# Attention scores of two heads made together, the keys' low parts as two 64-row matmuls side by side in the array

## The chip, the cores and the metric

The kernel runs on one core of one Trainium2 chip. The metric is device time in microseconds (us) of one execution; less is better. In the profile PE is TensorE's matmul, PEld its weight load, DVE is VectorE, ACT is ScalarE, POOL is GpSimd and SP is SyncE. L966 is line 966 of the kernel.

## The reference

One decoder layer on 512 tokens of width 1024, in float32: a norm, one wide input projection, two token mixers side by side (causal pooling, and sparse attention), a gated merge with an output projection, and an MLP with a squared ReLU. The change lies in the attention: 16 heads of 64 channels, eight heads to a group that shares its keys and values. Each query has three branches, each with a softmax of its own: compressed keys (31 of them), selected blocks of 64 keys, and a sliding window. With 512 tokens there are 8 blocks and up to 16 are picked, and the window is 512 long, so that both the selected and the window branch see every earlier key.

```python
def nsa_mixer(q, kc, vc, ks, vs, kw, vw, g_nsa, ...):
    q = apply_rope(q.reshape(B, S, N_HEADS, dh), cos, sin).reshape(B, S, G, HPG, dh)
    ks = apply_rope(ks.reshape(B, S, G, dh), cos, sin)
    kw = apply_rope(kw.reshape(B, S, G, dh), cos, sin)
    ...
        s_s = jnp.einsum('bqghd,bgqkd->bghqk', qb, k_sel) * scale
        p_s = masked_softmax(s_s, ok[:, :, None])
        o_s = jnp.einsum('bghqk,bgqkd->bqghd', p_s, v_sel)
    ...
        s_w = jnp.einsum('bqghd,bkgd->bghqk', qb, kwb) * scale
        p_w = masked_softmax(s_w, wmask)
        o_w = jnp.einsum('bghqk,bkgd->bqghd', p_w, vwb)
        o = gb[..., 0:1] * o_c + gb[..., 1:2] * o_s + gb[..., 2:3] * o_w
```

## The kernel before

Matmuls run in the fp32r format. To keep float32's accuracy, an operand is split into a high part (the value rounded to fp32r) and a low part (the rest), and a product is the sum of high x high, high x low and low x high.

The kernel has three stages. Up to about 180 us it makes the norm, the pooling mixer, the compressed keys and values and part of the input projection. Then comes the attention. Behind it come the merge, the output projection and the MLP. Line 377 and line 1339 are helpers that issue the big projections' matmuls. At about 73 us the compressed branch adds two small transposes of 64 rows (line 698) and some plain float32 matmuls (line 707); at about 123 us there are matmuls with 64 columns of weights (line 722). A transpose of 36 rows at about 24 us (line 802) turns a few small inputs.

**The attention's work unit is a slot.** There are 96: for each of 8 pairs of heads 12 slots, in a fixed order written out by the list `slots`. A slot holds the pair `p`, the branch `br`, a block `qb` of 128 queries and the head `h` of the pair (0 or 1). For the first two query blocks one slot takes both branches; for the last two each branch has its own slot. Slots 2k and 2k+1 differ only in `h`.

**How a score is made.** For a pair of heads the tile `Q[p]` has 128 partitions. For `h` = 0 its rows 0 to 63 hold the query's high part and rows 64 to 127 its low part; for `h` = 1 it is the other way round (`q_done`). `KH[g]` holds the keys' high parts twice, in rows 0 to 63 and in rows 64 to 127, and `KL[g]` the keys' low parts in the same way (`k_done`). So one 128-row matmul with `KH` gives (query high + query low) x key high, and a second one with `KL` adds (query high + query low) x key low in the same PSUM bank. `score_pe` issues the two one after the other, with 256, 384 or 512 columns.

**What follows a score.** `smax` (line 988, DVE) takes the masked score out of PSUM and finds the row's extreme, `expo` (line 998, ACT) exponentiates, `weight` (lines 1008 and 1011, DVE and POOL) divides by the sum and multiplies by the gate, `turn_pe` (line 1028, PE) transposes the weights four slots later, `turn_hi` (line 1039, ACT) and `turn_lo` (line 1043, DVE) split them, and `pv` (line 1062, PE) multiplies by the values two slots after that, once for each two slots.

**The order** is one loop over the slots. Slot `i` of the loop issues in turn: the score of slot `i + 1`, the transposes of slot `i - 4`, the maximum, exponential and weight work, a step of the generators in `side` (rope, the compressed scores), the filler's matmuls up to an even share (`fill`, the projections of line 377 with the tile `psF`), and every second slot a `pv`. Instructions stay in about that order on each engine.

**Banks.** Scores rotate through three PSUM banks (`tag="S"`, `S_BANKS` = 3). The compressed scores of the next pair (`cmp_scores`, tile `psC`), which join `side` at slot 3 of every twelve, take a bank of the same three.

Of the kernel before, what the change touches and what calls it, by code (L numbers as in the profile page):

```python
# [13 lines left out]
F32 = mybir.dt.float32  # L14
# [6 lines left out]
S = 512  # L21
# [5 lines left out]
S_BANKS, T_BANKS, F_BANKS = 3, 2, 2  # L27
# [35 lines left out]
def trunk(ctx: ExitStack, tc: tile.TileContext, A, out):  # L63
    nc = tc.nc
    PE, ACT, DVE, POOL = nc.tensor, nc.scalar, nc.vector, nc.gpsimd
    PSUM = bass.MemoryType.PSUM

    def pool(name, **kw):
        return tc.tile_pool(name=name, bufs=1, reuse_waits="tile", **kw)
# [107 lines left out]
    for c in range(4):  # L177
# [7 lines left out]
        if c < C_FF2:  # L185
# [3 lines left out]
            for o in OUT_TURN:  # L189
                g = seen.get(o, 0)  # L190
# [68 lines left out]
    def add_sum(behind=None):  # L259

        to, _, q = jobs[begun.popleft()]
        with tc.issue_after(behind.ins) if behind else nullcontext():
            POOL.dma_start(to, q, accum_op=ALU.add)  # L263
# [129 lines left out]
    def step_side():  # L393
        for _ in range(len(side)):
            g = side.popleft()
            try:
                next(g)
                side.append(g)
            except StopIteration:
                pass  # L400
# [64 lines left out]
    KH = [ap.tile([128, 4, 2, 128], FR, name=f"KH{g}") for g in range(2)]  # L465
    KL = [ap.tile([128, 4, 2, 128], FR, name=f"KL{g}") for g in range(2)]
# [94 lines left out]
    scored = {"pairs": 0, "rope": 0}  # L561
# [44 lines left out]
    Q = {}  # L606
# [13 lines left out]
    with ExitStack() as c1:  # L620
# [185 lines left out]
        for k in P1[2:]:  # L806
            i = int(k[-1]) if k[-1].isdigit() else None
# [35 lines left out]
    with ExitStack() as c2:  # L843
        p2 = c2.enter_context(pool("p2"))
        ps2 = c2.enter_context(pool("ps2", space=PSUM))
# [43 lines left out]
        def fill(n=1):  # L889
            for _ in range(n):  # L890
                if next(filler, True):
                    return False
                fdone[0] += 1
            return True
# [46 lines left out]
        slots = []  # L941
# [9 lines left out]
        live = {}  # L951
        PT = {}
        O = {}

        def score_pe(i):
            p, half, br, qb, h = slots[i]
            g = p // 4
            nb = qb + 1
            ps = ps2.tile([128, S], F32, tag="S", bufs=S_BANKS, name="psS")
            q = Q[p][:, h, 128 * qb:128 * qb + 128]  # L960
            for K, a in ((KH[g], True), (KL[g], False)):
                if half == 0:
                    rhs, n = K[:, 0:nb, :, :], 256 * nb
                else:
                    rhs, n = K[:, 0:nb, br, :], 128 * nb
                PE.matmul(ps[:, 0:n], q, rhs, start=a, stop=not a, skip_group_check=True)  # L966
            live[i] = ps

        def blocks(i):
            p, half, br, qb, h = slots[i]  # L970
# [5 lines left out]
        def smax(i):  # L976
            p, half, br, qb, h = slots[i]
            ps = live[i]
            sm = p2.tile([128, 3, 2], F32, tag="sm", bufs=6, name="sm")
            P = p2.tile([128, S], F32, tag="P", bufs=P_BUFS, name="P")  # L980
            for e, (b, o, nb) in enumerate(blocks(i)):
                n = 128 * nb
                if half == 0:
                    s = ps[:, 0:2 * n].rearrange("p (a b c) -> p a b c", b=2, c=128)[:, :, b, :]
                else:
                    s = ps[:, 0:n].rearrange("p (a c) -> p a c", c=128)
                m = cmask[:, S - n:].rearrange("p (a c) -> p a c", c=128)
                DVE.tensor_tensor_reduce(out=P[:, o:o + n].rearrange("p (a c) -> p a c", c=128), in0=s, in1=m,  # L988
                                         scale=1.0, scalar=3e38, op0=ALU.add, op1=ALU.min,
                                         accum_out=sm[:, 0, e:e + 1])  # L990
            live[i] = (ps, sm, P)

        def expo(i):
            p, half, br, qb, h = slots[i]
            ps, sm, P = live[i]
            for e, (b, o, nb) in enumerate(blocks(i)):
                c = P[:, o:o + 128 * nb]
                last_exp[:] = [ACT.activation(c, c, AF.Exp, bias=sm[:, 0, e:e + 1], scale=-1.0,  # L998
                                              accum_out=sm[:, 1, e:e + 1])]

        def weight(i):
            p, half, br, qb, h = slots[i]
            ps, sm, P = live[i]
            head = 2 * p + h
            bl = blocks(i)
            nb_ = len(bl)
            c = 3 * head + 1 + bl[0][0]
            DVE.reciprocal(sm[:, 2, 0:nb_], sm[:, 1, 0:nb_])  # L1008
            for e, (b, o, nb) in enumerate(bl):
                n = 128 * nb  # L1010
                r = POOL.tensor_scalar(P[:, o:o + n], P[:, o:o + n], sm[:, 2, e:e + 1],  # L1011
                                       GT[:, qb, c + e:c + e + 1], op0=ALU.mult, op1=ALU.mult)
            return r
# [8 lines left out]
        def turn_pe(i):  # L1022
            p, half, br, qb, h = slots[i]
            ps, sm, P = live[i]
            n = sum(b[2] for b in blocks(i))
            pt = ps2.tile([128, S], F32, tag="T", bufs=T_BANKS, name="psT")
            for j in range(n):
                PE.transpose(pt[:, 128 * j:128 * j + 128], P[:, 128 * j:128 * j + 128], ident)  # L1028
            live[i] = (pt, n)

        def turn_views(i):
            h = slots[i][4]
            pt, n = live[i]
            tH, tL = pt_tile(i)
            return pt[:, 0:128 * n].rearrange("p (a c) -> p a c", c=128), tH[:, 0:n, h, :], tL[:, 0:n, h, :]

        def turn_hi(i):
            src, dH, dL = turn_views(i)
            ACT.activation(dH, src, AF.Copy)  # L1039

        def turn_lo(i):
            src, dH, dL = turn_views(i)
            DVE.tensor_tensor(dL, src, dH.bitcast(F32), op=ALU.subtract)  # L1043
            live.pop(i)

        def pv(i):
            p, half, br, qb, h = slots[i]
            g = p // 4
            if (p, half) not in O:
                O[p, half] = [ps2.tile([128, 2, 2, 128], F32, tag="O", bufs=1, name="psO"), 2 if half == 0 else 4]  # L1050
                c = PTc[p]
                for h in range(2):
                    PE.matmul(O[p, half][0][:, :, h, :], VC[g][h], c[:, 256 * half:256 * half + 256],
                              start=h == 0, stop=False, skip_group_check=True)
            ps = O[p, half][0]
            O[p, half][1] -= 1
            last = O[p, half][1] == 0
            tH, tL = PT.pop((p, br, qb))
            kbs = [(b, k) for b in ((0, 1) if br is None else (br,)) for k in range(qb + 1)]
            for j, (b, k) in enumerate(kbs):  # L1060
                for t in (tH, tL):
                    PE.matmul(ps[:, qb % 2, :, :], VV[:, k, b, g, :], t[:, j, :, :], start=False,  # L1062
                              stop=last and j == len(kbs) - 1 and t is tL, skip_group_check=True)
            return last
# [15 lines left out]
        n = len(slots)  # L1080
        total = 4 * len(FILL2) + 4
        done0 = fdone[0]
        after = deque()
        score_pe(0)
        for i in range(n + LAG + PLAG):
            if i < n:
                p = slots[i][0]
                if i % 12 == 3 and p + 1 < NPAIR:
                    while p + 1 not in Q:
                        fill()  # L1090
                        step_side()
                if i % 12 == CMP_AT and p + 1 < NPAIR:
                    side.append(cmp_scores(p + 1))
            if i + 1 < n:
                score_pe(i + 1)
                scored["pairs"] = (i + 2) // 12
            t = i - LAG
            if 0 <= t < n:
                turn_pe(t)
                turn_hi(t)  # L1100
            if i < n:
                smax(i)
                expo(i)
            if 0 <= i - 1 < n:
                last = weight(i - 1)
            if i % 4 == 3 and len(begun) > 1:
                add_sum(last)
            if 0 <= t < n:
                turn_lo(t)
            step_side()  # L1110
            want = done0 + (total - done0) * (i + 1) // (n + LAG + PLAG)
            while fdone[0] < want and fill():
                pass
            if i < 5:
                fill()
            j = t - PLAG
            if 0 <= j < n and j % 2 == 1 and pv(j):
                o_evac(*slots[j][0:2])
# [368 lines left out]
    for c in range(4):  # L1487
# [16 lines left out]
        if c < C_FF2:  # L1504
            outs = [Out(c, h, Y) for h in range(2)]
            seen = {}
            for o in OUT_TURN:
                h = seen.get(o, 0)
# [61 lines left out]
```

## Time and profile before

| | |
|---|---|
| median of 3 runs | 826.72 us (826.69 to 827.03) |
| profiled execution | 825.73 us, span 824.0 us |
| PE busy | 792.6 us (96%), 5081 matmuls |
| DVE busy | 615.0 us (75%) |
| ACT busy | 483.5 us (59%) |
| POOL busy | 206.1 us (25%) |
| score matmuls (line 966) | 96 with high keys, 96 with low keys, from 186.2 to 378.0 us |

A row of the profile names the line, the engine and the operation, then the tile written and the tiles read, then the shape. For a matmul `128*128 128x512` stands for 128 rows and 128 columns of weights in the array and 512 streamed columns; `64*128` means that 64 rows of the array are used. Matmuls are pipelined: the duration of one runs from its start to the (modelled) end of its result, and in a stream the next one starts well before that. What one costs in a stream is the distance from its start to the next start.

### The profile page before, as it was taken

The page shows a single profiled execution, that of the slowest core. Times are in us where ns is not written, and L with a number is a line of the kernel's source. Part 1 is how long each engine was busy: PE and PEld are TensorE (multiplying, and loading weights), DVE is VectorE, ACT ScalarE, POOL GpSimd, SP SyncE. Part 2 cuts the span into 40 slices and gives each one's busy share as a digit, 9 for nine tenths or more (in the row PEclk, how much of TensorE's full clock was granted, in tenths as well). Part 3 has the DMA queues.
Part 4 walks back from the last instruction along what each step waited for, and adds up shares of the span by engine and source line. Part 5 has one row for each costly group of instructions (what it writes and reads, how often), then busy time and mean ns, then how long its engine had stood idle before and what let it go on. Part 6 is the DMA issues. An engine that isn't in the chain of part 4 may idle for free.

```text
span 824.0 us, 13915 instructions
## 1 busy us (share of the span) xinstructions
PE 792.6 (96%) x5081; PEld 708.5 (86%) x5081; DVE 615.0 (75%) x1201; ACT 483.5 (59%) x959; POOL 206.1 (25%) x271
## 2 busy tenths in 40 slices
PE   7999999998899999999999999999999999899996
PEld 5889878886788888888787889999999999899985
DVE  6797744549979988888554689986898689987823
ACT  5566433327778787899323585933782468347711
POOL 6000000027767866674234101101101010000000
PEclk9999999999999999999999999999999999999999
DMA  9363732357446624554955709969996785245402
GB/s 299 97 173 109 201 85 89 109 154 163 68 127 117 146 73 92 101 129 109 297 157 160 173 1 274 296 171 248 264 255 153 232 231 179 93 139 179 154 1 102
DMA packets 121277, 127.71 MB, mean 155 GB/s; under 512 B 5077, under 2 KB 109049, under 8 KB 121082
## 3 DMA queue, kind: packets, MB, share of 16 engines
q1 hardware_dynamic: 101914, 107.17, 40.5%
q0 software_dynamic: 19008, 18.88, 16.3%
q8 instruction: 40, 0.66, 0.3%
q10 hardware_dynamic: 288, 0.79, 0.3%
q14 instruction: 27, 0.22, 0.1%
HBM read 122.09 MB, written 39.85 MB: 197 GB/s over the span
## 4 chain that ended last, share of the span: by engine, by line
PE 71%; DVE 16%; ACT 5%; issue 3%; DMA 2%; POOL 1%; SPq 0%; DVEq 0%; ACTq 0%; POOLq 0%
PE psF L377 21%; PE psB L1339 16%; PE psB L377 12%; PE psB L1455 9%; PE psO L1062 3%; PE psT L1028 3%; PE psS L966 2%; DVE wl L291 2%; PE psV L377 2%; DVE P L988 2%; DVE PT L1043 1%; DMA raw<-w_out 1%; PE psF L431 1%; ACT P L998 1%; PE psC L666 1%
## 5 line engine op out<-in xcount | busy, mean ns | idle before, releaser
L377 PE MATMUL psF<-R,wh 128*128 128x512 f32 x512 | 166.6, 404 | 0.2 <-ACT MA L824 0.2
L289 ACT ACTIVATE wh<-raw 128x1024 fp32r<-128x1024 f32 x66 | 69.8, 1057 | 80.6 <-PE psB L1339 29.1
L334 ACT ACTIVATE wh<-raw 128x512 fp32r<-128x512 f32 (+1 forms) x102 | 61.3, 619 | 86.8 <-PE psF L377 35.8
L377 PEld LDWEIGHTS psF<-R,wh 128*128 128x128 f32 x512 | 92.4, 189 | 17.9 <-ACT MA L824 0.5
L377 PE MATMUL psF<-R,wl 128*128 128x512 f32 x256 | 101.6, 397 | 0.7 <-DVE wl L336 0.7
L1011 POOL TENSOR_SCALAR P<-P,sm,GT 128x128 f32<-128x128 f32 (+3 forms) x128 | 85.6, 700 | 46.6 <-DVE sm L1008 31.0
L291 DVE TENSOR_TENSOR wl<-raw,wh 128x1024 fp32r<-128x1024 f32 x66 | 80.6, 1221 | 20.1 <-ACT wh L289 19.5
L263 POOL DMA_DIRECT2D S<-w_ff x36 | 41.7, 1159 | 213.2 <-DMA S<-w_ff 162.0
L336 DVE TENSOR_TENSOR wl<-raw,wh 128x512 fp32r<-128x512 f32 (+1 forms) x78 | 56.1, 731 | 37.3 <-ACT wh L334 36.9
L998 ACT ACTIVATE P<-P,sm 128x128 f32<-128x128 f32 (+3 forms) x128 | 71.0, 557 | 11.2 <-DVE sm L988 10.1
L1339 PE MATMUL psB<-R,wh 128*128 128x256 f32 x352 | 64.1, 282 | 0.0
L988 DVE CUSTOM_DVE_ANT_0 P<-psS,cst 128x128 f32<-128x128 f32 (+3 forms) x128 | 59.6, 483 | 5.9 <-PE psT L1028 4.2
L336 POOL TENSOR_TENSOR wl<-raw,wh 128x512 fp32r<-128x512 f32 x28 | 39.9, 1428 | 84.3 <-ACT wh L334 82.0
L1043 DVE TENSOR_TENSOR PT<-psT,PT 128x512 fp32r<-128x512 f32 (+2 forms) x96 | 56.7, 594 | 4.1 <-ACT PT L1039 3.0
L377 PEld LDWEIGHTS psF<-R,wl 128*128 128x128 f32 x256 | 48.2, 188 | 11.9 <-DVE wl L336 0.9
L1039 ACT ACTIVATE PT<-psT 128x512 fp32r<-128x512 f32 (+2 forms) x96 | 49.2, 520 | 15.4 <-PE psT L1028 14.7
L289 ACT ACTIVATE w3h<-raw 128x1024 fp32r<-128x1024 f32 x32 | 33.8, 1057 | 40.5 <-PE psB L1455 14.4
L1028 PE MATMUL psT<-ident,P 128*128 128x128 f32 x320 | 51.3, 275 | 6.3 <-POOL P L1011 4.9
L1339 PEld LDWEIGHTS psB<-R,wh 128*128 128x128 f32 x352 | 54.1, 189 | 0.3 <-DVE R L1281 0.2
L1028 PEld LDWEIGHTS psT<-ident,P 128*128 128x128 f32 x320 | 39.6, 141 | 16.7 <-POOL P L1011 7.7
L291 DVE TENSOR_TENSOR w3l<-raw,w3h 128x1024 fp32r<-128x1024 f32 x32 | 39.1, 1222 | 14.6 <-ACT w3h L289 14.6
L1339 PE MATMUL psB<-R,wl 128*128 128x256 f32 x176 | 49.5, 281 | 0.0
(431 smaller groups left out, 2279.9 us busy)
## 6 DMA issues: line engine op xcount, KB each, us to landing
raw<-w_ff SPq DMA_DIRECT2D x50, 512.0 KB, 4.8
S<-w_ff POOLq DMA_DIRECT2D x36, 512.0 KB, 6.6
raw<-S SPq DMA_DIRECT2D x36, 512.0 KB, 4.4
raw<-w_in SPq DMA_DIRECT2D x32, 512.0 KB, 3.9
S<-w_ff SPq DMA_DIRECT2D x28, 512.0 KB, 5.3
S<-S SPq DMA_DIRECT2D x8, 512.0 KB, 8.2
raw<-w_proj_nsa SPq DMA_DIRECT2D x8, 512.0 KB, 4.1
raw<-w_out SPq DMA_DIRECT2D x8, 512.0 KB, 4.8
```

Of the source, the lines that this page charges most:

```text
L289: ACT.activation(h, t, AF.Copy)
L291: DVE.tensor_tensor(l, t, h.bitcast(F32), op=ALU.subtract)
L334: ACT.activation(h[:, sl], t[:, sl], AF.Copy)
L336: eng.tensor_tensor(l[:, sl], t[:, sl], h[:, sl].bitcast(F32), op=ALU.subtract)
L377: PE.matmul(ps, a, b, start=first and j == 0, stop=last and j == n - 1, skip_group_check=True)
L988: DVE.tensor_tensor_reduce(out=P[:, o:o + n].rearrange("p (a c) -> p a c", c=128), in0=s, in1=m, scale=1.0, scalar=3e38, op0=ALU.add, op1= ...
L998: last_exp[:] = [ACT.activation(c, c, AF.Exp, bias=sm[:, 0, e:e + 1], scale=-1.0, accum_out=sm[:, 1, e:e + 1])]
L1011: r = POOL.tensor_scalar(P[:, o:o + n], P[:, o:o + n], sm[:, 2, e:e + 1], GT[:, qb, c + e:c + e + 1], op0=ALU.mult, op1=ALU.mult)
L1028: PE.transpose(pt[:, 128 * j:128 * j + 128], P[:, 128 * j:128 * j + 128], ident)
L1043: DVE.tensor_tensor(dL, src, dH.bitcast(F32), op=ALU.subtract)
L1339: PE.matmul(out, w[u][:, k, 128 * f:128 * f + 128], XB[x][v][:, k, :], **kw)
L1455: PE.matmul(out, YB[y][u][:, k, 128 * f:128 * f + 128], w[v][:, k, :], **kw)
```

## The change

`score_pe` is split. `score_hi` issues the matmul with the keys' high parts as before, with all 128 rows. `score_lo` issues the matmul with the keys' low parts with 64 rows only: those 64 partitions that hold the high part of the head's query, rows 0 to 63 for `h` = 0 and rows 64 to 127 for `h` = 1. The product of the query's low part and the key's low part is no longer added. The two heads' low products use different halves of the array's rows and different PSUM banks.

The loop makes the scores of two slots at once, at every odd slot `i`: the high product of slot `i + 1`, then the transposes of slot `i - 4`, then the high product of slot `i + 2`, then the two low products one behind the other. At even slots no score is made. The number of banks is the same.

```diff
-        def score_pe(i):
+        def score_hi(i):
+
             p, half, br, qb, h = slots[i]
-            g = p // 4
+            ps = ps2.tile([128, S], F32, tag="S", bufs=S_BANKS, name="psS")
+            live[i] = ps, *keys(i)
+            PE.matmul(ps[:, 0:live[i][3]], Q[p][:, h, 128 * qb:128 * qb + 128], live[i][1], start=True, stop=False,
+                      skip_group_check=True)
+
+        def score_lo(i):
+
+            p, half, br, qb, h = slots[i]
+            ps, _, low, n = live[i]
+            r = slice(64 * h, 64 * h + 64)
+            PE.matmul(ps[:, 0:n], Q[p][r, h, 128 * qb:128 * qb + 128], low[r], start=False, stop=True,
+                      skip_group_check=True)
+            live[i] = ps
+
+        def keys(i):
+            p, half, br, qb, h = slots[i]
             nb = qb + 1
-            ps = ps2.tile([128, S], F32, tag="S", bufs=S_BANKS, name="psS")
-            q = Q[p][:, h, 128 * qb:128 * qb + 128]
-            for K, a in ((KH[g], True), (KL[g], False)):
-                if half == 0:
-                    rhs, n = K[:, 0:nb, :, :], 256 * nb
-                else:
-                    rhs, n = K[:, 0:nb, br, :], 128 * nb
-                PE.matmul(ps[:, 0:n], q, rhs, start=a, stop=not a, skip_group_check=True)
-            live[i] = ps
+            if half == 0:
+                return KH[p // 4][:, 0:nb, :, :], KL[p // 4][:, 0:nb, :, :], 256 * nb
+            return KH[p // 4][:, 0:nb, br, :], KL[p // 4][:, 0:nb, br, :], 128 * nb
...
-        score_pe(0)
+        for f in (score_hi, score_lo):
+            f(0)
+            f(1)
         for i in range(n + LAG + PLAG):
...
-            if i + 1 < n:
-                score_pe(i + 1)
-                scored["pairs"] = (i + 2) // 12
+            two = i % 2 == 1 and i + 1 < n
+            if two:
+                score_hi(i + 1)
             t = i - LAG
             if 0 <= t < n:
                 turn_pe(t)
                 turn_hi(t)
+            if two:
+                score_hi(i + 2)
+                score_lo(i + 1)
+                score_lo(i + 2)
+                scored["pairs"] = (i + 3) // 12
```

## The prediction

> **What bounds the kernel now.** I read the page first, then the busy time of the engines in the stretch where the scores are made, then the chain of work in that stretch, and last the timeline of the matmul engine around single instructions. From the page:
>
> ```profile
> PE 792.6 (96%) x5081; PEld 708.5 (86%) x5081; DVE 615.0 (75%) x1201; ACT 483.5 (59%) x959; POOL 206.1 (25%) x271
> PEclk9999999999999999999999999999999999999999
> ```
>
> The matmul engine (PE) is busy for 96% of 824.0 us, and its granted clock is nine tenths or more in every slice. The scores (line 966) are made between 186 and 378 us. Busy times there, in two windows (length; PE, weight load, DVE, ACT, POOL; clock; DMA share; GB/s), then the chain's first line in the second window, then the same windows for line 966 alone (PE, weight load):
>
> ```profile
> 186.00:240.00 54.00, 47.38 (x283) 39.72 (x282) 50.13 (x155) 41.33 (x117) 38.41 (x56) 0.97 0.49 100
> 240.00:380.00 140.00, 138.08 (x895) 121.42 (x894) 122.52 (x408) 118.03 (x318) 99.86 (x138) 1.00 0.52 114
> by line: PE psF L377 21.3%; PE psO L1062 13.7%; PE psS L966 12.4%; PE psT L1028 12.2%; DVE P L988 6.1%; issue 4.3%; DVE PT L1043 4.3%; ACT P L998 2.4%; DVE rx L586 2.2%; DVE oT L1071 2.1%; PE psO L1053 1.9%; DMA rs<-rx 1.7%; PE psC L903 1.7
> 186.00:240.00 54.00, 14.82 (x54) 8.61 (x54) 0.97 0.49 100
> 240.00:380.00 140.00, 39.52 (x138) 22.20 (x138) 1.00 0.52 114
> ```
>
> From 240 us on PE idles 1.9 us of 140, while DVE idles 17.5; PE's lines hold 63% of the chain. So there PE time is kernel time, nearly one for one. Before 240 us PE idles 6.6 us of 54, mostly for softmax weights, as in this row of the timeline (start, length, what; in brackets the idle time before and its releaser):
>
> ```profile
> 196.82 0.44 PE L1028 MATMUL psT<-ident,P 128*128 128x128 f32 x2 [2.16 <-POOL P L1011]
> ```
>
> There part of any PE time added goes into waits that are paid anyway.
>
> **What the change takes off PE.** The products with the keys' low parts, grouped by shape (count, busy, mean ns):
>
> ```profile
> L966 PE MATMUL psS<-KL,Q 128*128 128x512 f32 x48 | 18.9, 395 | 0.0
> L966 PE MATMUL psS<-KL,Q 128*128 128x384 f32 x32 | 10.8, 336 | 0.0
> L966 PE MATMUL psS<-KL,Q 128*128 128x256 f32 x16 | 4.5, 282 | 0.0
> ```
>
> These 96 become 48 pairs (24 of 512 columns, 16 of 384, 8 of 256), each pair two matmuls of 64 rows, one in the upper and one in the lower half of the array. A mean of 395 ns is the time until the result is out, not what one costs in a stream; that is the distance between starts:
>
> ```profile
> 249.70 0.39 PE L377 MATMUL psF<-R,wh 128*128 128x512 f32 x1
> 249.93 0.39 PE L377 MATMUL psF<-R,wl 128*128 128x512 f32 x1
> 252.17 0.33 PE L966 MATMUL psS<-KL,Q 128*128 128x384 f32 x1
> 252.34 0.27 PE L1028 MATMUL psT<-ident,P 128*128 128x128 f32 x1
> 285.95 0.29 PE L966 MATMUL psS<-KL,Q 128*128 128x256 f32 x1
> 286.07 0.49 PE L1028 MATMUL psT<-ident,P 128*128 128x128 f32 x3
> ```
>
> So 0.23, 0.17 and 0.12 us. Perfectly side by side, one of each pair vanishes: 24 x 0.23 + 16 x 0.17 + 8 x 0.12 = 5.52 + 2.72 + 0.96 = 9.2 us. That is the whole possible gain, 0.19 us a pair.
>
> **What it adds: a change of shape in the array, twice a pair.** All around the low products uses the full array: the high products before them, and behind them the next slot's transposes, a filler or the values' product. The trace has 64-row work between full-array work once without another wait: two transposes at 72.98 us. PE, then the weight loads (PEld):
>
> ```profile
> 72.61 0.30 PE L377 MATMUL psV<-wl,R 128*128 128x304 f32 x1
> 72.75 0.30 PE L377 MATMUL psV<-wh,R 128*128 128x304 f32 x1
> 72.98 0.34 PE L698 MATMUL psM<-ident,oT 64*128 64x64 f32 x2
> 73.25 0.41 PE L377 MATMUL psV<-wh,R 128*128 128x304 f32 x1
> 73.49 0.30 PE L377 MATMUL psV<-wl,R 128*128 128x304 f32 x1
> 72.98 0.20 PEld L698 LDWEIGHTS psM<-ident,oT 64*128 64x128 f32 x2 [0.18 <-issue]
> 73.24 0.19 PEld L377 LDWEIGHTS psV<-wh,R 128*128 128x128 f32 x1
> 73.35 0.19 PEld L377 LDWEIGHTS psV<-wl,R 128*128 128x128 f32 x1
> ```
>
> The 304-column matmuls follow each other at 0.14 us, so at 72.89 the array could have gone on; the 64-row work starts at 72.98: **0.09 us lost going in**. Its weights load at the same 72.98, not ahead as usual, so the first load lies open. The pair's row ends at 72.98 + 0.34 = 73.32, and one takes 0.22 us from start to end where its weights are there:
>
> ```profile
> L698 PE MATMUL psM<-ident,oT x4: 222/248/275, 73.0 to 111.1; 64*128 64x64 f32 x4
> L1028 PE MATMUL psT<-ident,P 128*128 128x128 f32 x320 | 51.3, 275 | 6.3 <-POOL P L1011 4.9
> ```
>
> So the second started at about 73.10. The three 128-column transposes of the row at 286.07 above take 0.49 where one takes 0.28 to its end, 0.11 each in the stream, so 64 columns take some 0.05 and the second had streamed by about 73.15. The next full weight load starts at 73.24: **0.09 us lost going out**. That load is open too: its matmul's record is 0.41 long instead of 0.30, and the next load starts **0.11 us** after it.
>
> The same stands at a 64-column matmul and at a 36-row transpose:
>
> ```profile
> 123.25 0.39 PE L377 MATMUL psF<-yd,wpl 128*128 128x512 f32 x1
> 123.57 0.45 PE L722 MATMUL psM<-oT,cg 128*64 128x64 f32 x4
> 123.94 0.74 PE L377 MATMUL psF<-R,wh 128*128 128x512 f32 x2
> 23.86 0.27 PE L431 MATMUL psF<-R,wl 128*128 128x256 f32 x1
> 24.07 0.25 PE L802 MATMUL psF<-ident,oT 36*128 36x36 f32 x1
> 24.25 0.51 PE L431 MATMUL psF<-R,wh 128*128 128x256 f32 x2
> ```
>
> 123.25 + 0.23 = 123.48 against 123.57; 23.86 + 0.12 = 23.98 against 24.07: 0.09 us both times. It is not plain float32 (these lines are not fp32r) that costs this, since a float32 matmul on the full array comes in at the ordinary distance:
>
> ```profile
> 74.89 0.30 PE L377 MATMUL psV<-wh,R 128*128 128x304 f32 x1
> 75.03 1.00 PE L707 MATMUL psM<-cg,w2d 128*128 128x64 f32 x8
> ```
>
> 74.89 + 0.14 = 75.03, nothing lost. The loss goes with the shape in use. The Trainium skill, "TensorEngine Tiling (Array Packing)", Tiling Modes, says that changing the tiling mode drains the engine and changing the tile within a mode does not; it gives no time for it, and the three places agree.
>
> **The sum.** A pair after the change: 0.09 in, 0.11 first low weights, 0.11 second low weights (the first product already streams), N for the second product, 0.09 out, 0.11 the next full weights; with N one product's stream this is 0.51 + N, against 2N now: 0.51 - N more. That is 0.28, 0.34 and 0.39 us: 24 x 0.28 + 16 x 0.34 + 8 x 0.39 = 6.7 + 5.4 + 3.1 = **15.2 us of PE time added**. The weights' 0.11 is that of full fp32r weights, the nearest row, since the low weights have as many columns.
>
> Bounds: if the second load is free (48 x 0.11 = 5.3 less), 9.9 us. If only the two losses count and no load lies open, 0.18 - N each: 15.2 - 48 x 0.33 = -0.6 us. If the two products do not overlap, 0.09 + 0.11 + 0.09 + 0.11 = 0.40 each, 19.2 us. I take 15.2, since the rows at 72.98 and at 73.24 both show the load open.
>
> How much reaches the end: 138 of the 192 score matmuls lie behind 240 us, 72% or 10.9 us; half of PE's 1.9 us idle takes up 1.0, leaving 9.9. The other 4.3 us meet the 6.6 us of waits before 240 us; I let half through, 2.1.
>
> **The order of scores, and a new wait.** High scores of two slots are now started at every odd slot, with the three banks unchanged: the second needs the bank of the slot before the current one, and behind the compressed scores (psC, every twelfth slot), which take a bank too, that of the current slot, whose maximum (line 988) is still to come. The sharpest case in the steady part is slot 53:
>
> ```profile
> 297.20 1.19 PE L1062 MATMUL psO<-PT,VV 128*128 128x256 f32 x8
> 297.94 0.55 DVE L988 CUSTOM_DVE_ANT_0 P<-psS,cst 128x384 f32<-128x384 f32 x1
> ```
>
> The new high score would stand where the first row starts; its bank is free at 298.49: 1.3 us, with the low products, fillers and values' products queued behind it on PE, and ACT and DVE waiting for those in turn. Seven such places at most make 9.1 us; nothing is lost where DVE is earlier, and a later PE makes DVE earlier. A gain is excluded, since no wait goes. I take 1.0 us. What the low products no longer sum (the query's low part times the key's low part) is in the same matmul and frees nothing else. DVE, ACT, POOL and the DMAs keep their instructions.
>
> Total: 9.9 + 2.1 + 1.0 = 13.0 us on the profiled execution's 825.73, 838.7. The median of the runs is 826.72, 0.99 above it, so **839.7 us**.
>
> **Rivals.** *Side by side at no cost (faster).* The Trainium skill, "TensorE: Matmul & The Clock Gate", Part 3, has packed matmuls start about 4 ns apart and cites 3.07 times for four row tiles. As a mechanism here: no loss at the borders, one product per pair hidden, 9.2 us off PE; 6.6 lie behind 240 us, where DVE's 17.5 us of slack is enough for three quarters, 5 us: 821.7. It decides where a pair's borders cost under 0.19 us. Against it stand three places with 0.09 us on the way in alone; for it, that none of them is an fp32r product. Chance 0.12.
>
> *Borders drain, loads hidden (no change).* -0.6 us and up to 1.0 of bank waits: 827. Against it: all loads behind a border lie open. Chance 0.07.
>
> *No overlap (slower still).* 19.2 us: 0.72 x 19.2 - 1.0 + 2.7 + 1.0 = 16.5, 843.2. Nothing in the trace has two products in different halves, so nothing refutes it. Chance 0.13.
>
> *Second load free.* 9.9 us: 7.1 - 1.0 + 1.4 + 1.0 = 8.5, 835.2. Chance 0.16. The forecast keeps 0.52.
>
> **The numbers.** Low end: the 9.9 us with all 1.9 us of idle used, nothing from before 240 us and no bank wait, 7.1 - 1.9 = 5.2: 832. High end: no overlap, nothing absorbed, 19.2 + 1.0: 847. This leaves out the first two rivals, 0.19. A measurement of this kernel can tell 0.2%, 1.7 us, from no change. Slower 0.52 + 0.13 + 0.16 = 0.81, same 0.07, faster 0.12.
>
> **What would show it.** Right: before each first low product a start 0.09 us later than the product ahead allows, its weights loading at the same moment; the second low product starting about 0.11 us behind the first; behind the pair an open load; PE's other groups unchanged, and the stretch from 240 us to the last score about 10 us longer. Wrong: low weights loaded ahead of the high products' end, both low products starting within some ns, and the full product behind them without a gap; or PE idling before high scores for DVE's line 988, which would make the banks the cost.

## The result, and the profile after

| | before | changed |
|---|---|---|
| median | 826.88 us (826.69 to 827.1) | 835.02 us (833.49 to 835.74) |
| profiled execution | 825.73 us, span 824.0 | 835.74 us, span 834.0 |
| ratio | | 1.0096, 95% interval 1.0078 to 1.0113 |

The change makes the kernel 8.1 us slower. A second measurement beside other runs gave 1.0078 (1.0059 to 1.0096). The prediction was 13.0 us slower, 839.7 us, with a range from 832 to 847 us that holds the measured time.

From the page of the changed kernel, busy times and granted clock:

```profile
PE 808.6 (97%) x5081; PEld 707.0 (85%) x5081; DVE 613.9 (74%) x1201; ACT 482.4 (58%) x959; POOL 207.6 (25%) x271
PEclk9999999998999999999999999999999999999999
```

PE has the same 5081 matmuls and 16 us more busy time; DVE, ACT and POOL are as busy as before. The same two windows as in the prediction, and the chain's first line in the second:

```profile
186.00:240.00 54.00, 52.07 (x253) 36.78 (x254) 45.77 (x143) 37.67 (x104) 36.79 (x52) 0.94 0.49 102
240.00:380.00 140.00, 139.92 (x871) 114.85 (x869) 115.98 (x396) 112.28 (x309) 98.41 (x138) 1.00 0.50 108
by line: PE psF L377 34.5%; PE psO L1072 20.7%; PE psT L1038 17.6%; PE psS L968 9.8%; PE psS L960 9.6%; PE psC L903 3.7%; PE psO L1063 2.6%; PE psT L936 1.8%; issue 0.1%
```

From 240 to 380 us PE idles 0.1 us and holds the whole chain; before, DVE, ACT and a DMA had their shares in it. In the same 140 us only 871 matmuls run, against 895.

Now the low products (line 968; the high ones are line 960). One pair in the timeline, PE and then the weight loads:

```profile
310.28 0.47 PE L960 MATMUL psS<-KH,Q 128*128 128x512 f32 x1
310.68 0.50 PE L968 MATMUL psS<-KL,Q 64*128 64x512 f32 x2
311.11 0.50 PE L377 MATMUL psF<-R,wh 128*128 128x512 f32 x1
310.68 0.19 PEld L968 LDWEIGHTS psS<-KL,Q 64*128 64x128 f32 x2 [0.24 <-issue]
311.11 0.30 PEld L377 LDWEIGHTS psF<-R,wh 128*128 128x128 f32 x2 [0.24 <-issue]
```

Two products of 512 columns take 0.50 us from the first start to the last end: they run together, and their two weight loads (0.19 us for both) do too. Nothing loads ahead on either side (the two idle times of 0.24 us), and the next full matmul starts 0.43 us after the pair. That 0.43 is 0.11 for the load, 0.23 for one stream and 0.09 going out. In front of the pair the high product takes 0.40 to the pair's start; with full rows, in the rows at 311.45 under "Order only", it takes 0.32, so that the way in shows here too. The trace has 36 such pairs. The other 24 low products stand alone, as here:

```profile
301.84 0.49 PE L968 MATMUL psS<-KL,Q 64*128 64x512 f32 x1
302.26 0.39 PE L1072 MATMUL psO<-PT,VV 128*128 128x256 f32 x1
302.49 0.39 PE L960 MATMUL psS<-KH,Q 128*128 128x512 f32 x1
302.81 0.50 PE L968 MATMUL psS<-KL,Q 64*128 64x512 f32 x1
303.24 0.39 PE L1072 MATMUL psO<-PT,VV 128*128 128x256 f32 x1
302.26 0.19 PEld L1072 LDWEIGHTS psO<-PT,VV 128*128 128x128 f32 x1 [0.24 <-issue]
302.37 0.19 PEld L960 LDWEIGHTS psS<-KH,Q 128*128 128x128 f32 x1
```

The passage in and out is paid here for each: the high product from 302.49 has streamed by 302.72 and the low one starts at 302.81 (0.09 in), takes the same 0.43 to the next start at 303.24, and the full load behind a passage lasts 0.11 (302.26 to 302.37). So **a passage costs 0.09 + 0.11 + 0.09 + 0.11 = 0.40 us beside the stream itself, whether one product or two use it.**

The kernel's source asks for 48 pairs. The scheduler that orders the program parted 12 of them: there it moved the first low product ahead of the second high product. Probably that product's bank was not free in its plan; no run shows the reason. Line 968 by window shows where (PE busy and count, then weight load):

```profile
186.00:240.00 54.00, 11.36 (x26) 4.47 (x26) 0.94 0.49 102
240.00:390.00 150.00, 16.74 (x70) 6.70 (x70) 1.00 0.49 104
```

Of the 26 low products before 240 us, 22 are single; of the 70 behind it, 2.

### The profile page after: what moved, and what is told of

It is laid out like the page before. It is cut to its first block, busy times and chain, and to the rows that moved or that the text cites. A ratio compares the mean times of both kernels' runs of the same rounds, so it can differ in the third digit from the quotient of the medians.

```text
span 834.0 us, 13931 instructions
## 1 busy us (share of the span) xinstructions
PE 808.6 (97%) x5081; PEld 707.0 (85%) x5081; DVE 613.9 (74%) x1201; ACT 482.4 (58%) x959; POOL 207.6 (25%) x271
## 4 chain that ended last, share of the span: by engine, by line
PE 80%; DVE 12%; issue 2%; ACT 2%; DMA 2%; POOL 2%; POOLq 0%; ACTq 0%; DVEq 0%; SPq 0%
PE psF L377 24%; PE psB L1356 16%; PE psB L377 12%; PE psB L1472 9%; PE psO L1072 4%; PE psT L1038 4%; PE psS L968 3%; PE psS L960 2%; DVE wl L291 2%; PE psV L377 2%; DMA raw<-w_out 1%; PE psF L431 1%; PE psC L666 1%; DVE w3l L291 1%; DVE x L515 1%
## 5 line engine op out<-in xcount | busy, mean ns | idle before, releaser
L289 ACT ACTIVATE w3h<-raw 128x1024 fp32r<-128x1024 f32 x32 | 33.8, 1057 | 41.9 <-PE psB L1472 15.8
L1072 PE MATMUL psO<-PT,VV 128*128 128x256 f32 x320 | 50.8, 291 | 0.0
```

The costliest lines, as they stand in the source:

```text
L289: ACT.activation(h, t, AF.Copy)
```

## The experiments

Ratios are against runs of the kernel before on the same chip; us is the ratio's distance from 1 times 827. The last column is the start of the first matmul into `psB`, where the stage behind the attention begins, in the profiled execution.

| kernel | ratio (95% interval) | us | clock, this / before | us at equal clock | `psB` begins |
|---|---|---|---|---|---|
| before | | | | | 397.9 |
| changed | 1.0096 (1.0078 to 1.0113) | +7.9 | 0.9925 / not listed | | 406.2 |
| order only, 128 rows | 0.9974 (0.9955 to 0.9993) | -2.2 | 0.9932 / 0.9922 | -1.4 | 397.2 |
| 64 rows only, old order | 1.0264 (1.0230 to 1.0297) | +21.8 | 0.9952 / 0.9922 | +24.1 | 420.2 |
| kept together | 1.0062 (1.0041 to 1.0083) | +5.1 | 0.9906 / 0.9922 | +3.9 | 404.5 |
| same half | 1.0154 (1.0118 to 1.0190) | +12.7 | 0.9932 / 0.9922 | +13.3 | 409.9 |
| low twice, kept together | 1.0191 (1.0165 to 1.0217) | +15.8 | 0.9938 / 0.9916 | +17.6 | 414.9 |
| no low products | 0.9948 (0.9927 to 0.9968) | -4.3 | 0.9876 / 0.9916 | -7.6 | 390.1 |
| order kept, 128 rows | 0.9991 (0.9977 to 1.0005) | -0.7 | 0.9929 / 0.9916 | +0.3 | 398.7 |
| order only, again | 0.9965 (0.9951 to 0.9979) | -2.9 | 0.9943 / 0.9916 | -0.5 | 395.9 |
| changed, again | 1.0078 (1.0059 to 1.0096) | +6.5 | 0.9938 / 0.9920 | +8.2 | 406.0 |
| two at once, plain | 0.9980 (0.9965 to 0.9996) | -1.7 | 0.9932 / 0.9920 | -0.5 | 397.7 |

The clock is the granted clock of the runs, averaged over the runs of the kernel and of the kernel before beside it. It matters at the size of these effects: among the 143 runs listed with a clock, 0.001 less of it goes with 0.64 us more in runs of one and the same kernel. "At equal clock" is an estimate: each run's time times its clock, averaged, less the same for the kernel before. It takes the whole time to stretch with the clock, so it corrects a little too much; its 95% interval is 0.7 to 1.3 us to each side, 2.6 for same half. What gives a kernel a higher or lower clock is not shown.

**Order only.** The changed kernel with full low products; its instructions stand in the changed kernel's order on every engine, so that the rows are the only difference.

```diff
-            PE.matmul(ps[:, 0:n], Q[p][r, h, 128 * qb:128 * qb + 128], low[r], start=False, stop=True,
+            PE.matmul(ps[:, 0:n], Q[p][:, h, 128 * qb:128 * qb + 128], low, start=False, stop=True,
```

> The changed kernel with one edit: the low products use all 128 rows again; every engine's instructions stand in the order of the changed kernel. Theory A (each passage of the array from 128 rows to 64 and back costs about 0.40 us of PE): nothing is left of the cost, so 825 to 829 us, since what remains is the new order of scores. Rival B (making two scores at once in three banks is what costs, since PE waits for banks): still 833 to 837 us. Rival C (the two halves of the cost are alike): about 831 us.

2.2 us faster than the kernel before. B falls: order and banks cost nothing. The same window and chain as above, then a pair with full rows, at the place of the pair at 310.68 in the changed kernel:

```profile
240.00:380.00 140.00, 137.72 (x890) 122.29 (x889) 122.76 (x413) 118.48 (x322) 99.59 (x136) 1.00 0.52 109
by line: PE psF L377 21.2%; PE psO L1072 13.3%; PE psT L1038 11.9%; PE psS L960 6.1%; PE psS L968 5.8%; DVE P L998 4.6%; ACT P L1008 4.5%; DVE PT L1053 4.3%; issue 3.7%; ACT PT L1049 3.1%; DVE rx L586 2.2%; PE psC L903 1.9%; POOL rs L581 1.
311.45 0.48 PE L960 MATMUL psS<-KH,Q 128*128 128x512 f32 x1
311.77 0.62 PE L968 MATMUL psS<-KL,Q 128*128 128x512 f32 x2
312.24 0.61 PE L377 MATMUL psF<-R,wh 128*128 128x512 f32 x2
```

The two low products take 0.47 to the next start, two streams, and no load lies open behind them. That the high product takes 0.32 and not one stream, 0.23, comes from its own load, which lies open behind the transposes here and in the changed kernel (its record is 0.48 and 0.47 long instead of 0.39). PE idles 2.3 us again and the chain is shared again. From this kernel to the changed one nothing differs but passages and overlap, since the traces of both hold the same instructions in the same order on every engine: 1.0 to 1.3%, 9 to 11 us, of which some 9 remain at equal clock.

**64 rows only.** The kernel before with 64 rows in each low product, all else in its place.

```diff
-                PE.matmul(ps[:, 0:n], q, rhs, start=a, stop=not a, skip_group_check=True)
+                r = slice(0, 128) if a else slice(64 * h, 64 * h + 64)
+                PE.matmul(ps[:, 0:n], q[r], rhs[r], start=a, stop=not a, skip_group_check=True)
```

> The kernel before with one edit: the low product of each slot uses 64 rows (the query's low part times the key's low part is left out), each slot still alone and in the old order. Theory A: 96 single passages of 0.40 us are 38.9 us of PE time; 72% of it, 28 us, lies behind 240 us and shows whole, of the other 11 us a half to all, so 858 to 866 us. Rival B: the order is untouched, so 825 to 829 us. Rival D (64-row matmuls cost nothing by themselves, it is the pair in one array that is slow): 825 to 829 us as well.

21.8 us slower: the passages alone do it, with no new order. It is less than I expected. One place in the timeline:

```profile
349.77 0.28 PE L967 MATMUL psS<-KH,Q 128*128 128x256 f32 x1
349.98 0.38 PE L967 MATMUL psS<-KL,Q 64*128 64x256 f32 x1
350.29 0.55 PE L1029 MATMUL psT<-ident,P 128*128 128x128 f32 x3
```

349.77 + 0.12 = 349.89 against 349.98: 0.09 in. The start behind comes 0.31 after the low product's, 0.11 + 0.12 + 0.08. But the three transposes behind take 0.55 from first start to last end where the row at 286.07 in the prediction has 0.49, so that their open load costs 0.06, not 0.11. A passage before transposes is 0.34 to 0.35 us, and 79 of the 96 low products stand before transposes. With 0.40 for the other 17 the passages come to some 34 us, of which 22 reach the end (24 at equal clock).

**Kept together.** The changed kernel with no pair parted.

```diff
...
-                score_hi(i + 2)
-                score_lo(i + 1)
+                high = score_hi(i + 2)
+                with tc.issue_after(high.ins):
+                    score_lo(i + 1)
```

What is left out makes `score_hi` return its matmul.

> The changed kernel with one edit: the first low product is queued behind the second high product, so that all 48 pairs of low products stand next to each other (in the changed kernel the program has 36 pairs and 24 single ones, 11 of the 12 parted pairs ahead of 240 us). Theory A: 12 passages fewer at 0.40 us and 12 products of 0.12 to 0.23 us hidden, 7 us of PE time, mostly ahead of 240 us where PE also waits for others, so half of it shows: 830 to 833 us. Rival B: holding the first low product back lets PE wait longer for banks: 835 to 840 us.

1.0062, 5.1 us above the kernel before, 2.8 us less than the changed kernel's first ratio and 1.3 less than its second. Its interval overlaps with both of theirs, so the times alone don't show the gain. But this kernel had the lower clock (0.9906 against 0.9925 and 0.9938); at equal clock it is 3.9 us above the kernel before and the changed one 8.2, which makes the gain about 4 us.

**Same half.** Both low products in rows 0 to 63, in the changed kernel's order.

```diff
-            r = slice(64 * h, 64 * h + 64)
+            r = slice(0, 64)
```

> The changed kernel with one edit: both low products use rows 0 to 63, so that they can't lie side by side (for the second head these rows hold the query's low part, so its scores differ); the order of instructions is that of the changed kernel. Theory A with overlap: the 36 pairs lose what was hidden, one stream each (0.23, 0.17 or 0.12 us, 6.9 us in all) and up to 0.11 us for a second weight load, 34 of them behind 240 us: 841 to 846 us. If the products did not overlap in the changed kernel: 834 to 836 us.

12.7 us above the kernel before, 4.8 to 6.2 above the changed kernel, close under the forecast with overlap and clear of the one without. The overlap is real. A pair now:

```profile
336.49 0.48 PE L960 MATMUL psS<-KH,Q 128*128 128x512 f32 x1
336.90 0.73 PE L968 MATMUL psS<-KL,Q 64*128 64x512 f32 x2
337.56 0.50 PE L1072 MATMUL psO<-PT,VV 128*128 128x256 f32 x2
```

The pair takes 0.73 instead of 0.50 and the next start 0.66 instead of 0.43: one stream more, 0.23, and no second load or passage. `psB` begins 3.7 us later than in the changed kernel, though this trace kept its full clock through the attention, where the changed one lost 3.4 us of clock (see the last section). The two together, 7.1 us, are what the 36 pairs had hidden, 6.9 us.

**Low twice.** The kept-together kernel with the pair issued twice in each passage.

```diff
...
-                    score_lo(i + 1)
-                score_lo(i + 2)
+                    score_lo(i + 1, False)
+                    score_lo(i + 2, False)
+                    score_lo(i + 1)
+                score_lo(i + 2)
```

What is left out gives `score_lo` its second argument; `False` keeps the sum in the bank open.

> The kernel with the pairs kept together, with one edit: in each of 47 passages the pair of low products is issued twice (the low product counts double in the scores). The second pair needs no passage; its weights can load under the first pair. Theory A (the passage is paid once, not per matmul): one stream more per pair, 9.1 us of PE time, of which 5 to 8 us show: 5 to 8 us above the kept-together kernel. If each 64-row pair paid its own 0.40 us: 28 us more of PE time, 15 to 22 us above it.

```profile
302.91 0.42 PE L960 MATMUL psS<-KH,Q 128*128 128x384 f32 x1
303.26 0.62 PE L968 MATMUL psS<-KL,Q 64*128 64x384 f32 x4
303.81 0.41 PE L903 MATMUL psC<-KC,Q 128*128 128x64 f32 x2
303.26 0.30 PEld L968 LDWEIGHTS psS<-KL,Q 64*128 64x128 f32 x4 [0.18 <-issue]
```

Four products of 384 columns take 0.62 from start to end and 0.55 to the next start: 0.11 + 2 x 0.17 + 0.09 = 0.54. The second pair costs its stream alone; the passage is paid once. Two passages would take at least 2 x 0.37 = 0.74. In time the kernel is 10.7 us above the kept-together one (13.7 at equal clock), more than the 5 to 8 I expected. 9.1 us of it are streams. The rest fits the waits: the order changed too, and from 240 to 380 us PE is busy for 135.54 us of the 140, against 139.83 in the kept-together kernel, 4.3 us less. Its longest waits there (total, times, longest):

```profile
PE psO L1064 <- ACT P L1009: 2.0, 1, 2.0
PE psC L903 <- DVE sm L999: 1.2, 1, 1.2
PE psS L960 <- DVE sm L999: 0.4, 1, 0.4
```

The first is a wait for the softmax. The other two, 1.6 us, are waits for `smax` to free a score bank.

**No low products.** The kernel before without its 96 low products.

```diff
-            for K, a in ((KH[g], True), (KL[g], False)):
+            for K, a in ((KH[g], True),):
...
-                PE.matmul(ps[:, 0:n], q, rhs, start=a, stop=not a, skip_group_check=True)
+                PE.matmul(ps[:, 0:n], q, rhs, start=True, stop=True, skip_group_check=True)
```

> The kernel before without the 96 low products (the keys' low parts are left out of the scores). It measures what PE time is worth in this stage: 18.4 us of streams go (48 x 0.23 + 32 x 0.17 + 16 x 0.12). If PE alone set the stage's end, 72% of it, 13 us, would show behind 240 us: 812 to 815 us. If PE and the softmax chain on DVE, ACT and POOL are close to each other, half of that: 819 to 822 us. If the chain set it: 825 to 828 us.

4.3 us faster for 18.4 us of streams less. By the start of `psB` the gain is 7.8 us, and 3.5 of it are lost later. That is the clock: behind the start of `psB` this trace has two more stretches at half clock than the kernel before, with 0.57 granted from 390 to 394 and from 537 to 541 us, 1.7 us lost in each. The runs say the same: their clock is 0.9876 on average against 0.9916, and at equal clock the kernel is 7.6 us faster. The attention stage from 240 us on:

```profile
240.00:380.00 140.00, 133.90 (x867) 115.56 (x866) 125.29 (x419) 122.08 (x329) 104.72 (x140) 1.00 0.54 119
by line: ACT P L998 15.6%; ACT PT L1039 11.7%; PE psF L377 10.9%; issue 9.0%; PE psO L1062 5.2%; PE psT L1028 4.9%; DVE PT L1043 3.7%; DVE P L988 3.7%; ACT wh L334 3.7%; DMA rs<-rx 3.6%; ACT ot L1069 3.4%; ACT R L876 3.1%; PE psS L966 2.3%;
```

ACT's exponential and split take the head of the chain, and PE idles 6.1 us. So the softmax chain lies close behind PE: of the 18.4 us taken off PE less than half shows, 7.6 to 7.8 us without the loss of clock and 4.3 with it.

**Order kept.** The kept-together kernel with full low products, the same edit as in order only; the order is the kept-together kernel's on every engine.

> The kernel with the pairs kept together, with one edit: the low products use all 128 rows; the order is that of the kept-together kernel. Theory A: no passage, so 5 to 9 us less than the kept-together kernel, level with the order-only kernel, 824 to 828 us. It is also the candidate for a kernel faster than both. If what the kept-together kernel loses is waiting for banks: within 2 us of it.

-0.7 us, with 1 in the interval. It is 5.9 us faster than the kept-together kernel (1.0062 against 0.9991), 3.6 at equal clock: that is what reaches the end of the 48 passages, 24 x 0.17 + 16 x 0.23 + 8 x 0.28 = 10.0 us of PE time. It is 2 us slower than the order-only kernel beside it, but 1.2 us of that is clock (0.9929 against 0.9943). So whether holding the low products back costs time isn't shown.

**Order only, again.**

> The order-only kernel once more, in more rounds, beside the kept-together order: it was 0.26% faster than the kernel before, with an interval of 0.07 to 0.45%. If that is real: 0.9955 to 0.999 of the kernel before. If not: an interval that holds 1.

0.9965: a gain of 0.21 to 0.49%. In time it beats both the kernel before and the changed one. Of its 2.9 us over the kernel before, though, some 2.2 are clock (0.9943 against 0.9916), and what is left at equal clock, 0.5 us, is not clear of noise; in the first measurement 1.4 us were left. The two profiles show one place for a real gain: between 186 and 240 us, at the same granted clock of 0.97, PE is busy for 49.45 and 49.76 us against 47.38 in the kernel before, and runs 289 and 293 matmuls against 283. So some 2 us of waits go there.

**Changed, again.**

> The changed kernel once more, on the chip and beside the runs of the kernel before that the next kernel shares, for a tighter ratio against the order-only kernel. Its own earlier ratio was 1.0096: 1.008 to 1.011 again, which leaves 1.2 to 1.3% or 10 to 11 us between it and the order-only kernel (0.9965 to 0.9974), the share of 17.3 us of passages that reaches the end.

1.0078, a little under what I expected, though at equal clock it is 8.2 us. The trace again has 36 pairs and 24 single products.

**Two at once, plain.** The order-only kernel with each slot's two products together.

```diff
             if two:
                 score_hi(i + 1)
+                score_lo(i + 1)
...
                 score_hi(i + 2)
-                score_lo(i + 1)
                 score_lo(i + 2)
```

> The order-only kernel with one edit: at an odd slot the high and the low product of a slot follow each other (high, low, transposes, high, low) instead of both low products at the end; all with 128 rows. If making two scores at once is what made the order-only kernel faster: 0.995 to 0.999 of the kernel before. If it was holding the low products back behind the transposes: 0.999 to 1.002.

0.9980 (0.9965 to 0.9996): making two scores at once is faster by itself as measured, but 1.2 of the 1.7 us are clock. Whether holding the low products back adds to it, these runs can't tell.

## Why the prediction was right, and where its terms were off

**The passages: right.** The 0.09 us in, 0.09 out and the open loads of 0.11, read from two transposes at 73 us, are what the low products show (with 0.06 for the load behind, where transposes follow), and each experiment that takes passages away (order only, order kept) or adds them (64 rows only) moves the time that way. That the 64-row work at 73 us was plain float32 and not fp32r didn't matter. The rival without overlap falls with the same-half kernel. The Trainium skill's rule on changing the tiling mode ("TensorEngine Tiling (Array Packing)", Tiling Modes) says that a change of mode drains the engine and a change of tile within a mode does not. The traces agree in the cost, though they don't show what takes the time: the change costs 0.09 us each way, and the second pair of the low-twice kernel, which changes the tile inside one mode, costs no passage. The Trainium skill, "TensorE: Matmul & The Clock Gate", Part 3, has packed matmuls start some 4 ns apart. The traces agree here too: the two products of a pair start 3 to 4 ns apart in all 36 pairs.

**The second weight load: wrong.** The sum put 0.11 us a pair on it. The loads of the two halves run together, 0.19 us for both, so that a pair costs 0.40 - N more than before, not 0.51 - N. Among its signs of being wrong the prediction had both low products starting within some ns, and that one came; the others, weights loaded ahead and no gap behind the pair, did not. This is the rival "second load free", whose 835.2 stands beside the measured 835.02. Its price was right, 9.9 us of PE time for 48 pairs, but the agreement with the time is luck. The kernel that has 48 pairs is the kept-together one, and that is 5.1 us above the kernel before, not 8.5.

**The pairs that aren't: missed.** The sum took 48 pairs. With 36 pairs (18 of 512 columns, 12 of 384, 6 of 256) and 24 single products, PE's added time is 18 x 0.17 + 12 x 0.23 + 6 x 0.28 + 24 x 0.40 = 7.5 + 9.6 = 17.1 us. The free load took 0.11 x 48 = 5.3 us off the 15.2, the parted pairs put some 7 on again. That the sum of 15.2 lies so near 17.1 is luck: two errors in it nearly cancel.

**What reaches the end: less than forecast.** I let 12.0 of 15.2 us through, 79%: all but 1.0 behind 240 us and half of it before. Measured are 9 to 11 us of 17.1, 53 to 64%, between the order-only kernel and the changed one. Much of this follows from where the passages lie: 22 single ones and two pairs, 9.3 us of PE time, stand before 240 us, where PE also waits for softmax weights. By the prediction's own rule 17.1 us would give 7.8 - 1.0 + 4.65 = 11.5, a little above what was measured. Which waits take up the rest is not shown. Against the kernel before, the last score starts at 383.6 us instead of 378.0, 5.6 us later and not the 10 that were named as a sign; against the two order-only kernels it is 9 to 10 us later.

**The new wait: not there, and the order: a small gain.** I put 1.0 us on banks. In the changed kernel PE never waits for a score bank from 186 to 400 us. The bank probably shows in the order of the program instead, where the scheduler parted pairs; keeping them together gives 1.3 to 2.8 us back as measured, about 4 at equal clock. And I excluded a gain from the new order because no wait goes. Some 2 us of waits before 240 us do go; order only is 2.2 to 2.9 us faster, of which 0.5 to 1.4 remain at equal clock.

**The faster rival: likely too dear.** It gave 5 us to a free overlap, which takes 9.2 us off PE. Taking away 18.4 us brought 4.3 us, or 7.6 at equal clock; at that share 9.2 us would bring 2 to 4. No run takes off just 9.2. "PE time is kernel time" held for a good half of the time added and for a quarter to two fifths of the time removed.

## What to carry to other kernels

Matmuls on half of the array's rows do run side by side here, loads included, but going from full-array work to them and back cost 0.40 us, and one hidden 512-column stream is worth 0.23. By these numbers such work saves PE time only if at least two pairs of 512 columns, or three of 384, share one passage; no run here shows a gain from it. Where a bank or buffer decides whether two instructions can stand together, look at the order that the scheduler made and not at the source. A stage in which PE is 98% busy can still give back less than half of what is taken off PE: see who holds the chain once PE's time is taken out, before pricing a gain. And compare the granted clocks before explaining a difference of 0.3%: here a third to four fifths of such a gain went with the clock.

## What the runs showed of the hardware that I had not expected

Early in the stage PE waits some 2 us for softmax weights in the kernel before and in the changed one. In the changed kernel the granted clock then falls to half for about 7 us (windows of 4 us; the clock is the third number from the end):

```profile
194.00:198.00 4.00, 2.39 (x14) 1.63 (x14) 4.00 (x3) 0.70 (x2) 4.00 (x8) 1.00 0.86 120
198.00:202.00 4.00, 3.76 (x13) 2.30 (x13) 3.83 (x12) 2.47 (x6) 2.53 (x5) 0.73 0.44 144
202.00:206.00 4.00, 4.00 (x10) 2.39 (x11) 2.52 (x10) 1.76 (x6) 2.54 (x4) 0.50 0.64 82
206.00:210.00 4.00, 4.00 (x23) 3.24 (x23) 3.27 (x8) 3.90 (x9) 2.59 (x4) 0.92 0.33 54
```

That is 0.27 x 4 + 0.50 x 4 + 0.08 x 4 = 3.4 us of clock lost. The kernel before kept its clock there and fell to 0.80 and 0.78 from 218 to 226 us, 1.7 us lost. The order-only kernel lost 1.7 us in each of its two profiles and the changed kernel 3.4 in each of its two, while PE was busy at half clock with hardly a break. So 1.7 of the 9.0 and 10.1 us by which `psB` begins later in the changed kernel than in the order-only one are clock and not passages. Over whole executions it evens out: the changed kernel's runs had no lower clock than those of the kernel before (0.9925 and 0.9938 against 0.9916 to 0.9922), so the clock doesn't explain why it is slower. Two kernels without passages, order kept and two at once, also lost 3.4 us in this stage in their profiles. The kernel with 64 rows only, which has the most passages, kept the full clock all through the stage, so passages by themselves don't lower it; what lowers it, and for how long, is open.
